# Matmuls that take their moving columns alternately from two halves

## The chip, the core and the metric

The kernel runs on one core of one Trainium2 chip. The metric is the device time of one execution in microseconds (us); the median of several runs is compared. TensorE (PE) does matrix products: a stationary operand of up to 128 x 128 (the weights here) is loaded, a moving operand (the activations here) streams past it column by column, and the result goes to PSUM, which has eight banks of 512 fp32 columns. VectorE (DVE) and ScalarE (ACT) read PSUM banks and read and write SBUF. GpSimd (POOL) and SyncE (SP) mostly issue transfers.

## What is computed

One inference step of a decoder with two layers, for a prompt of 512 positions and for 8 samples of one position each. All 520 positions go through the same weights, so they are handled together. Cut to what matters here:

```
def _swiglu(x, wg, wu, wd):
    return (jax.nn.silu(x @ wg) * (x @ wu)) @ wd          # 1024 -> 2816 -> 1024

for l in range(DEPTH):                                     # DEPTH = 2
    if l == N_A_LAYERS:                                    # after the first layer
        kv = _rmsnorm(x, kv_norm_g) @ w_kv                 # shared keys and values
    x = x + 0.5 * _swiglu(_rmsnorm(x, norm_g[l, 0]), ...)
    h = _rmsnorm(x, norm_g[l, 1])
    x = x + (pooling mixer(h) if l < N_A_LAYERS else window attention(h @ w_q) @ w_o)
    x = x + 0.5 * _swiglu(_rmsnorm(x, norm_g[l, 2]), ...)
y = _rmsnorm(x, final_norm_g)
```

There are four feed-forward blocks. They hold most of the arithmetic.

## The kernel before

**Layout.** Activations lie transposed: 128 features on the partitions, the 520 positions (`TOK`) as columns in the free dimension, eight such tiles for 1024 features. `H` is 260, half of the columns; `hcols(t, 0)` and `hcols(t, 1)` are the first and the second 260 columns of a tile. A pair of PSUM banks (`duo()`) takes a tile of 520 results, 260 in each bank, and `halves(t)` views an SBUF tile in the same two halves.

**Products.** Every operand is split into a high and a low part of type fp32r, and each product is the sum of three matmuls: high by high, low by high, high by low (`terms`). Two helpers issue nearly all of them:

- `mm` (matmuls at L604) multiplies one block of 128 x 128 weights with one activation tile, three terms by two halves of 260 columns. It serves the plain tiles, the projections of queries, keys, values and outputs, and the plain down products.
- `product` (matmuls at L632) multiplies four blocks of weights with four pieces of 260 columns, twelve matmuls into one bank. It serves the Strassen-like form, in which a block of products over two halves of the features and two halves of the columns is made from seven products of sums, not from eight.

In both, the moving operand `b` is a run of 260 adjacent fp32r columns in SBUF, the result a run of 260 adjacent columns at the start of a bank (`bank[:, :H]`). The names of the moving operands in the profile are `xh`/`xl`, `th`/`tl`, `hh`/`hl` and `ph`/`pl` (high and low parts), those of the split weights `wh`/`wl`, those of the banks `ps`. Some products do not go through these helpers: the pooling mixer (L1193, L1238), the attention scores and values (L1533, L1618), the tail of the last block (264 columns at L1970, 384 at L1977) and transposes (L1880, L1591 and others).

**Who reads the banks.** In `plain_end` VectorE multiplies gate sums by the norm factor `R` (L751), ScalarE applies silu, and VectorE multiplies with the up sums (L753). In `strassen_tile` ScalarE copies intermediate sums (`sa`, `sb`: L775, L780, L783) and VectorE adds and multiplies from banks (L787, L793, L798); `strassen_down` does likewise (L812 to L838). `add` inside `ffn` (L908) adds a plain down product to the residual, `o_add` (L1761) the output projection, `rope` and `q_evac` (L1474) copy keys and queries, L1376 the values.

**Order.** Weights are loaded in chunks by SP's and POOL's queues, split by ScalarE (`wh`, L287) and VectorE (`wl`, L288), and prefetched a few pieces ahead (`Weights`). Outside the attention part, where a written plan sets the order, a scheduler places the instructions of each engine.

Of the kernel before, what the change touches and what calls it, by code (L numbers as in the profile page):

```python
# [324 lines left out]
def yoco_step(ctx, tc, ins, outs):  # L325
# [212 lines left out]
    def halves(t):  # L538
        return t.rearrange("p (h c) -> p h c", h=2)

# [59 lines left out]
    def mm(w, kk, mov, banks, first, last, halves=(0, 1), pin=seq, between=None):  # L600

        for i, (a, b) in enumerate(terms(w, mov)):
            for hf in halves:
                ins = T.matmul(  # L604
                    banks[:, hf, :H],
                    a[:, kk, :],
                    hcols(b, hf),
                    start=(first and i == 0),
                    stop=(last and i == 2),
                )  # L610
                pin(ins)
            if between is not None and i < 2:
                between()
# [11 lines left out]
    def product(mov, bank, more=False):  # L625


        w = W.get()
        W.prefetch()
        for kk in range(4):  # L630
            for i, (a, b) in enumerate(terms(w, mov[kk])):
                T.matmul(  # L632
                    bank[:, :H],
                    a[:, kk, :],
                    b,
                    start=(not more and kk == 0 and i == 0),
                    stop=(kk == 3 and i == 2),
                    skip_group_check=more,
                )
# [95 lines left out]
    def plain_end(tmp, pg, pu, hs):  # L735
# [3 lines left out]
        if not there[0]:  # L739
            S.copy(halves(g), pg[:, :, :H])  # L740
            S.copy(halves(t), pu[:, :, :H])

# [7 lines left out]
        else:  # L750
            V.tensor_tensor(halves(g), pg[:, :, :H], halves(R), op=ALU.mult)  # L751
            S.activation(t, g, AF.Silu)
            V.scalar_tensor_tensor(halves(g), pu[:, :, :H], -1.0, halves(t), op0=ALU.mult, op1=ALU.mult)  # L753
            hidden(g, hs)
# [7 lines left out]
    def strassen_tile(tmp, xx, tt, hs, early=False):  # L762
# [11 lines left out]
        product(B(xx, lo, 0), a)  # L774
        S.copy(hcols(sa, 0), a[:, :H])  # L775
# [4 lines left out]
        S.copy(sb, b[:, :H])  # L780
        finish()
        product(B(tt, lo, 1), a, True)
        S.copy(hcols(sa, 1), a[:, :H])  # L783
# [3 lines left out]
        V.tensor_tensor(halves(g), halves(sa), c[:, :, :H], op=ALU.add)  # L787
        if early:
# [3 lines left out]
        product(B(tt, up, 0), a, True)  # L792
        V.tensor_tensor(sb, sb, a[:, :H], op=ALU.add)  # L793

        def rest():
            V.tensor_tensor(hcols(g, 1), sb, hcols(t, 1), op=ALU.mult)
            product(B(tt, up, 1), a, True)
            V.tensor_tensor(hcols(g, 0), a[:, :H], hcols(t, 0), op=ALU.mult)  # L798
            hidden(g, hs)
# [3 lines left out]
    def strassen_down(tmp, hs):  # L803
# [3 lines left out]
        def head(i):  # L807
# [3 lines left out]
            product(b["B11"], a)  # L811
            S.copy(hcols(sa, 0), a[:, :H])  # L812
            product(b["T1"], c[:, 1, :])
            S.copy(sb, c[:, 1, :H])
            st[i] = a, c, sa, sb

        def second(i):
            a, c, sa, sb = st[i]
            product(b["T2"], a, True)
            S.copy(hcols(sa, 1), a[:, :H])  # L820

        def third(i):
# [3 lines left out]
            u = tmp.tile([P, TOK], F32, tag="u", name="u", bufs=nu[0])  # L826
            V.tensor_tensor(halves(u), halves(sa), c[:, :, :H], op=ALU.add)
# [3 lines left out]
            V.tensor_tensor(sb, sb, a[:, :H], op=ALU.add)  # L831

        def rest(i):
# [3 lines left out]
            product(b["T4"], a, True)  # L837
            V.tensor_tensor(hcols(u, 0), a[:, :H], hcols(R, 0), op=ALU.mult)  # L838
            V.scalar_tensor_tensor(x[2 * i + 1], u, 0.5, x[2 * i + 1], op0=ALU.mult, op1=ALU.add)
# [39 lines left out]
    def ffn(fi, tmp, mov, hooks, tt, tags, after, before_last=None, first=None, by_parts=None, hold=False):  # L879

        j = 0
        for pi, n in enumerate(PARTS):
# [20 lines left out]
            def add(m, bank, hfs):  # L903
                c = slice(hfs[0] * H, (hfs[-1] + 1) * H)
                u = tmp.tile([P, TOK], F32, tag="u", name="u", bufs=nu[0])[:, c]
                parts = lambda z: z.rearrange("p (h c) -> p h c", c=H)
                pin = later if last and hold and m >= PIN0 else seq
                pin(V.tensor_tensor(parts(u), bank[:, hfs[0] : hfs[-1] + 1, :H], parts(R[:, c]), op=ALU.mult))  # L908
                pin(V.scalar_tensor_tensor(x[m][:, c], u, -0.5, x[m][:, c], op0=ALU.mult, op1=ALU.add))
# [407 lines left out]
    def rope(out, banks, cosr, sinr, pool, tags):  # L1317
# [3 lines left out]
        sw = pool.tile([P, TOK], F32, tag=tags[1], name="rp1", bufs=n)  # L1321
        S.copy(halves(raw), banks[:, :, :H])
        V.tensor_tensor(out, raw, cosr, op=ALU.mult)
# [5 lines left out]
    with ff_pool() as tmp:  # L1329
# [45 lines left out]
        for g in range(2):  # L1375
            V.tensor_tensor(halves(vT[g]), vb[g][:, :, :H], halves(R), op=ALU.mult)  # L1376

# [70 lines left out]
    with tc.tile_pool(name="at", bufs=2, reuse_waits="tile") as at:  # L1448
# [22 lines left out]
        def q_evac(t):  # L1471

            qraw[t] = big.tile([P, TOK], F32, tag="th", name="qraw")
            later(S.copy(halves(qraw[t]), qb[t][:, :, :H]))  # L1474

# [283 lines left out]
        def o_add(n):  # L1759
            half, m = n // KT, n % KT  # L1760
            later(V.tensor_tensor(halves(x[m]), parts.pop((half, m))[:, :, :H], halves(x[m]), op=ALU.add))  # L1761

# [333 lines left out]
```

## Time and profile before

| | |
|---|---|
| median of 3 runs | 1617.17 us (1616.67 to 1617.82) |
| span of the profiled execution, first to last instruction | 1614.7 us |
| own time of the profiled execution beyond its span | not given apart; the median lies 2.5 us above the span |
| TensorE | 1599.9 us busy, 13338 matmuls |
| weight loads of TensorE | 1589.5 us, 13338 |
| VectorE | 1417.0 us |
| ScalarE | 976.4 us |
| GpSimd | 310.0 us |

Matmuls overlap in a pipeline, so their printed durations (some 283 ns) are longer than the distance from one to the next; the distance is read from the chain of work in order of time. "PEld" is the weight load, which overlaps the matmul before it. A row of a group gives line, engine, operation, output <- inputs, shapes and count, then busy time and the mean duration in ns, then the idle time of the engine just before and who ended it.

### The profile page before, as it was taken

To read this page: it belongs to the slowest core of one execution; us is meant where nothing else is said; L and a number is where in the kernel's file an instruction comes from. 1 tells how busy PE (TensorE), PEld (TensorE's weight loads), DVE (VectorE), ACT (ScalarE), POOL (GpSimd) and SP (SyncE) were. 2 spreads that over 40 slices of the span, in tenths; PEclk is the share of its full clock that TensorE was granted. 3 is DMA by queue.
4 is the path that set the end of the run, shared out by engine and by line. 5 is a ranking of instruction groups with operands and counts; after the bars stand their busy time and mean duration, and the time that the engine had idled before them with its cause. 6 is when DMAs were issued, how large, how long until landed. Compare 5 with 4: busy or idle time off the path is not lost.

```text
span 1614.7 us, 35073 instructions
## 1 busy us (share of the span) xinstructions
PE 1599.9 (99%) x13338; PEld 1589.5 (98%) x13338; DVE 1417.0 (88%) x2783; ACT 976.4 (60%) x2030; POOL 310.0 (19%) x348
## 2 busy tenths in 40 slices
PE   9999999999999999999999999999999999999997
PEld 9999999999999999999999999999999999999997
DVE  6999999879999999978899999877787999999976
ACT  5765665657665665655565565555786665565555
POOL 1122222101121221100312222200461122222200
PEclk9999999999999999999999999999999999999999
DMA  9588888654687888735788878853333588888941
GB/s 236 115 187 184 181 180 189 162 171 119 131 188 169 186 182 182 168 114 120 192 175 180 189 172 181 193 159 90 67 85 91 121 169 184 185 183 182 190 123 54
DMA packets 420037, 255.43 MB, mean 158 GB/s; under 512 B 13182, under 2 KB 400246, under 8 KB 419828
## 3 DMA queue, kind: packets, MB, share of 16 engines
q1 hardware_dynamic: 339918, 187.56, 42.0%
q0 software_dynamic: 76192, 60.53, 26.1%
q10 hardware_dynamic: 3758, 5.09, 1.0%
q8 instruction: 105, 1.72, 0.4%
q14 instruction: 64, 0.52, 0.1%
HBM read 218.59 MB, written 6.11 MB: 139 GB/s over the span
## 4 chain that ended last, share of the span: by engine, by line
PE 98%; DVE 1%; ACT 0%; POOL 0%; issue 0%; DVEq 0%; ACTq 0%; POOLq 0%
PE ps L632 68%; PE ps L604 23%; PE pv L1618 1%; PE pv L1193 1%; PE pv L1591 1%; PE pv L1238 1%; PE ps L1533 1%; PE ps L1970 0%; PE ps L1977 0%; PE ps L1065 0%; PE ps L560 0%; PE pv L1724 0%; PE ps L1074 0%; ACT wh L287 0%; PE ps L1880 0%; PE pv L1678 0%
## 5 line engine op out<-in xcount | busy, mean ns | idle before, releaser
L287 ACT ACTIVATE wh<-raw 128x512 fp32r<-128x512 f32 (+1 forms) x770 | 449.2, 619 | 260.9 <-PE ps L632 76.9
L288 DVE TENSOR_TENSOR wl<-raw,wh 128x512 fp32r<-128x512 f32 (+1 forms) x770 | 500.8, 674 | 58.8 <-ACT wh L287 57.5
L632 PE MATMUL ps<-th,wh 128*128 128x260 f32 x1232 | 347.3, 283 | 0.4 <-ACT sb L780 0.4
L632 PE MATMUL ps<-tl,wh 128*128 128x260 f32 x1232 | 347.1, 283 | 0.0
L632 PE MATMUL ps<-th,wl 128*128 128x260 f32 x1232 | 345.8, 282 | 0.0
L632 PE MATMUL ps<-xh,wh 128*128 128x260 f32 x908 | 255.4, 283 | 0.8 <-ACT wh L287 0.7
L632 PE MATMUL ps<-xl,wh 128*128 128x260 f32 x908 | 254.6, 282 | 0.0
L632 PE MATMUL ps<-xh,wl 128*128 128x260 f32 x908 | 254.2, 282 | 0.0
L632 PEld LDWEIGHTS ps<-th,wh 128*128 128x128 f32 x1232 | 231.9, 188 | 1.1 <-ACT sb L780 0.6
L632 PEld LDWEIGHTS ps<-tl,wh 128*128 128x128 f32 x1232 | 231.8, 188 | 0.0
L632 PEld LDWEIGHTS ps<-th,wl 128*128 128x128 f32 x1232 | 231.1, 188 | 0.0
L398 POOL DMA_DIRECT2D S<-in_ffn_w_up_dram x77 | 102.2, 1327 | 472.6 <-DMA S<-in_ffn_w_up_dram 139.4
L632 PE MATMUL ps<-hh,wh 128*128 128x260 f32 x656 | 183.9, 283 | 1.6 <-ACT wh L287 0.7
L632 PE MATMUL ps<-hl,wh 128*128 128x260 f32 x656 | 184.1, 283 | 0.0
L632 PE MATMUL ps<-hh,wl 128*128 128x260 f32 x656 | 183.2, 282 | 0.0
L214 POOL DMA_DIRECT2D raw<-raw x109 | 96.2, 882 | 401.2 <-DVE wl L288 127.2
L632 PEld LDWEIGHTS ps<-xh,wh 128*128 128x128 f32 x908 | 170.4, 188 | 1.6 <-ACT wh L287 1.6
L632 PEld LDWEIGHTS ps<-xl,wh 128*128 128x128 f32 x908 | 170.6, 188 | 0.0
L632 PEld LDWEIGHTS ps<-xh,wl 128*128 128x128 f32 x908 | 170.4, 188 | 0.0
L632 PEld LDWEIGHTS ps<-hh,wh 128*128 128x128 f32 x656 | 122.9, 188 | 2.7 <-ACT wh L287 1.1
L632 PEld LDWEIGHTS ps<-hl,wh 128*128 128x128 f32 x656 | 123.2, 188 | 0.1
L632 PEld LDWEIGHTS ps<-hh,wl 128*128 128x128 f32 x656 | 122.9, 188 | 0.0
(369 smaller groups left out, 3639.8 us busy)
## 6 DMA issues: line engine op xcount, KB each, us to landing
raw<-in_ffn_w_gate_dram SPq DMA_DIRECT2D x87, 512.0 KB, 4.4
raw<-in_ffn_w_up_dram SPq DMA_DIRECT2D x87, 512.0 KB, 5.9
raw<-in_ffn_w_down_dram SPq DMA_DIRECT2D x128, 256.0 KB, 4.8
raw<-raw POOLq DMA_DIRECT2D x109, 256.0 KB, 3.8
S<-in_ffn_w_up_dram SPq DMA_DIRECT2D x77, 256.0 KB, 4.2
S<-in_ffn_w_up_dram POOLq DMA_DIRECT2D x77, 256.0 KB, 5.4
raw<-in_ffn_w_down_dram SPq DMA_DIRECT2D x16, 768.0 KB, 4.4
S<-in_ffn_w_down_dram SPq DMA_DIRECT2D x32, 256.0 KB, 3.2
```

The lines of the kernel that those rows point to most:

```text
L214: G.dma_start(blk(raw, 2, 1), blk(raw, 1, 1), accum_op=ALU.add)
L287: pin(nc.scalar.activation(dh, src, AF.Copy))
L288: pin(nc.vector.tensor_tensor(dl, src, dh.bitcast(F32), op=ALU.subtract))
L398: return [ld(lambda t: t, a), lambda t: nc.gpsimd.dma_start(t, b, accum_op=ALU.add)]
L604: ins = T.matmul(banks[:, hf, :H], a[:, kk, :], hcols(b, hf), start=(first and i == 0), stop=(last and i == 2),)
L632: T.matmul(bank[:, :H], a[:, kk, :], b, start=(not more and kk == 0 and i == 0), stop=(kk == 3 and i == 2), skip_group_check=more,)
L1193: later(T.matmul(o, a[:, c], b[:, kk, :], start=(n == 0), stop=(n == 5)))
L1238: later(T.matmul(o, zz[tau][z][:, c], b, start=(i == 0), stop=(i == len(lst) - 1)))
L1533: later(T.matmul(o, q_[rows, qc], k_[rows, kc_], start=(i == 0), stop=(i == 2)))
L1591: later(T.transpose(self.both[bi][:, kt * 256 + e * P : kt * 256 + (e + 1) * P], z, ident))
L1618: later(T.matmul(o, a, p_[:, kc_], start=(n == 0), stop=(n == 3 * len(kts) - 1)))
```

## The change

The products of `mm` and `product` take their moving columns in another order: column 0, 130, 1, 131 and so on of the 260, through a view of two dimensions (`two`). Their results still go to 260 adjacent columns of a bank, so result column 2a + b belongs to position 130b + a. All readers of these banks take them back in the order of positions: they read the bank with a step of two columns, first the even and then the odd ones (`outs` for a pair of banks, `out` for one), and write SBUF in the usual order; `back` and the new `halves` give the SBUF views the matching dimensions. Products outside the two helpers are as before.

```
 def halves(t):
-    return t.rearrange("p (h c) -> p h c", h=2)
+    return t.rearrange("p (h b a) -> p h b a", h=2, b=2)
+
+def two(z):
+    return z.rearrange("p (b a) -> p a b", b=2)
+
+def back(z):
+    return z.rearrange("p (b a) -> p b a", b=2)
+
+def outs(banks):
+    return banks[:, :, :H].rearrange("p h (a b) -> p h b a", b=2)
+
+def out(bank):
+    return bank[:, :H].rearrange("p (a b) -> p b a", b=2)
...
     # mm
                     banks[:, hf, :H],
                     a[:, kk, :],
-                    hcols(b, hf),
+                    two(hcols(b, hf)),
...
     # product
                     bank[:, :H],
                     a[:, kk, :],
-                    b,
+                    two(b),
...
     # plain_end
-            V.tensor_tensor(halves(g), pg[:, :, :H], halves(R), op=ALU.mult)
+            V.tensor_tensor(halves(g), outs(pg), halves(R), op=ALU.mult)
             S.activation(t, g, AF.Silu)
-            V.scalar_tensor_tensor(halves(g), pu[:, :, :H], -1.0, halves(t), op0=ALU.mult, op1=ALU.mult)
+            for hf in range(2):
+                V.scalar_tensor_tensor(
+                    back(hcols(g, hf)), out(pu[:, hf, :]), -1.0, back(hcols(t, hf)), op0=ALU.mult, op1=ALU.mult
+                )
...
     # strassen_tile
-        S.copy(hcols(sa, 0), a[:, :H])
+        S.copy(back(hcols(sa, 0)), out(a))
...
-        V.tensor_tensor(halves(g), halves(sa), c[:, :, :H], op=ALU.add)
+        V.tensor_tensor(halves(g), halves(sa), outs(c), op=ALU.add)
...
-        V.tensor_tensor(sb, sb, a[:, :H], op=ALU.add)
+        V.tensor_tensor(back(sb), back(sb), out(a), op=ALU.add)
```

The other readers of these banks (`strassen_down`, `add`, `rope`, the values, `q_evac`, `o_add`) change in the same way.

The instructions are the same in kind and number but for one: the product at L753 (`scalar_tensor_tensor`) is issued as two of 260 columns each. On VectorE, at the end of the third plain tile of the first feed-forward block (`g` is the gate tile, `t` its silu, `wl` the low part of a piece of weights, `xa`/`xb` and `t_...` the sums for the Strassen form), the rows before are:

```order
L288 TENSOR_TENSOR wl<-raw_362,wh 128x512
L751 TENSOR_TENSOR g<-ps_584,R 128x520
L380 TENSOR_TENSOR pl<-t_634,ph 128x520
L227 TENSOR_TENSOR raw_362<-raw_362 128x512
L873 TENSOR_TENSOR t_681<-xb,xa 128x260
L874 SCALAR_TENSOR_TENSOR t_681<-t_680,xb 128x260
L753 SCALAR_TENSOR_TENSOR g<-ps_585,t 128x520
```

The same place on VectorE after the change:

```order
L288 TENSOR_TENSOR wl<-raw_362,wh 128x512
L767 TENSOR_TENSOR g<-ps_584,R 128x520
L380 TENSOR_TENSOR pl<-t_634,ph 128x520
L227 TENSOR_TENSOR raw_362<-raw_362 128x512
L892 TENSOR_TENSOR t_681<-xb,xa 128x260
L893 SCALAR_TENSOR_TENSOR t_681<-t_680,xb 128x260
L770 SCALAR_TENSOR_TENSOR g<-ps_585,t 128x260 x2
```

The order stands; the last row has become two instructions of half the size.

The scheduler also places some ready instructions of neighbouring tiles in another order. The largest such place on TensorE lies in the Strassen tiles of the last feed-forward block (the numbers after `ps` name pairs of banks, and those of after are 8 higher for the same pair). Before:

```order
L632 MATMUL ps_18284<-th,wh 128x260
L632 MATMUL ps_18284<-tl,wh 128x260
L632 MATMUL ps_18284<-th,wl 128x260
L632 MATMUL ps_18403<-xh,wh 128x260
L632 MATMUL ps_18403<-xl,wh 128x260
L632 MATMUL ps_18545<-xh,wh 128x260
L632 MATMUL ps_18545<-xl,wh 128x260
L632 MATMUL ps_18403<-xh,wl 128x260
```

And in the changed kernel, at the place where the products for the pair 18411 end and the last products for the pair 18292 have not begun:

```order
L648 MATMUL ps_18411<-xh,wh 128x260
L648 MATMUL ps_18411<-xl,wh 128x260
L648 MATMUL ps_18410<-th,wh 128x260
L648 MATMUL ps_18410<-tl,wh 128x260
L648 MATMUL ps_18411<-xh,wl 128x260
```

Twelve matmuls into an older bank (18284, later 18292), which stood ahead of the end of the product into 18403 (now 18411), now stand behind it, and the first two of a product into 18410 have come ahead of that end. SP and POOL issue the same instructions in the same order as before.

More of the change, by code (lines that the diff above doesn't have):

```diff
@@ L819, in second @@
             product(b["T2"], a, True)
-            S.copy(hcols(sa, 1), a[:, :H])
+            S.copy(back(hcols(sa, 1)), out(a))
         def third(i):
@@ L1321, in rope @@
         sw = pool.tile([P, TOK], F32, tag=tags[1], name="rp1", bufs=n)
-        S.copy(halves(raw), banks[:, :, :H])
+        S.copy(halves(raw), outs(banks))
         V.tensor_tensor(out, raw, cosr, op=ALU.mult)
@@ L1473, in q_evac @@
             qraw[t] = big.tile([P, TOK], F32, tag="th", name="qraw")
-            later(S.copy(halves(qraw[t]), qb[t][:, :, :H]))
+            later(S.copy(halves(qraw[t]), outs(qb[t])))
         def q_gather(t, e):
```

27 lines of the change are left out of this document (13 added, 14 removed).

## The prediction

> **What bounds the kernel now.** I read the engines' shares first, then the chain of work that ended last, then the groups of instructions, then the chain in order of time at a few places, and last the busy time by stage.
>
> ```profile
> span 1614.7 us, 35073 instructions
> PE 1599.9 (99%) x13338; PEld 1589.5 (98%) x13338; DVE 1417.0 (88%) x2783; ACT 976.4 (60%) x2030; POOL 310.0 (19%) x348
> PEclk9999999999999999999999999999999999999999
> PE 98%; DVE 1%; ACT 0%; POOL 0%; issue 0%; DVEq 0%; ACTq 0%; POOLq 0%
> ```
>
> TensorE is busy in all but 14.8 us of the span, at a granted clock of nine tenths or more in every slice, and it is 98% of the chain. So the time is the number of matmuls times the distance from one matmul to the next. The busy sum cannot give that distance, since matmuls overlap: the groups below print 283 ns each. Their counts are of use. Each row stands for one of three terms with the same count (high by high, low by high, high by low part).
>
> ```profile
> L632 PE MATMUL ps<-th,wh 128*128 128x260 f32 x1232 | 347.3, 283 | 0.4 <-ACT sb L780 0.4
> L632 PE MATMUL ps<-xh,wh 128*128 128x260 f32 x908 | 255.4, 283 | 0.8 <-ACT wh L287 0.7
> L632 PE MATMUL ps<-hh,wh 128*128 128x260 f32 x656 | 183.9, 283 | 1.6 <-ACT wh L287 0.7 <-ACT hh L379 0.5 <-ACT sa L812 0.4
> L632 PE MATMUL ps<-ph,wh 128*128 128x260 f32 x256 | 72.7, 284 | 0.0
> L604 PE MATMUL ps<-hh,wh 128*128 128x260 f32 x572 | 116.5, 286 | 0.8 <-DVE g L751 0.6 <-DVE nm L1552 0.2
> L604 PE MATMUL ps<-xh,wh 128*128 128x260 f32 x448 | 91.1, 286 | 0.0
> ```
>
> That is 3 x (1232 + 908 + 656 + 256 + 572 + 448) = 12216 matmuls of 260 columns, of 13338 in all. These are the ones whose moving operand changes. The last column shows that they hardly wait for anyone: 3.6 us over these rows.
>
> The distance comes from the chain in order of time (start, length, what, how many):
>
> ```profile
> 108.12 143.90 PE ps L632 x1195
> 1579.12 4.30 PE ps L604 x36
> 1583.41 0.44 PE ps L1880 x4
> 1589.45 2.19 PE ps L1970 x18
> 1598.21 3.13 PE ps L1977 x18
> ```
>
> In the long stretch a matmul of 260 columns comes every 143.90/1195 = 120.4 ns (a few records may be missing, so it is a little less), in the short one every 119.4 ns. Those of 264 columns (L1970) take 121.7 ns, those of 384 columns (L1977) 173.9 ns. One more column thus costs (173.9 - 121.7)/120 = 0.435 ns, and 260 columns cost 113.1 of the 119.4 ns; the other 6.3 ns do not depend on columns. The transposes of 128 columns (L1880) come every 110 ns, not at half the distance: something apart from the columns, which goes with each matmul and its load of weights, keeps them 110 ns apart. The kernel is bounded by the rate at which columns stream, with that second floor 9.4 ns below.
>
> **The change part by part.** Counts of matmuls, columns, weight loads and transfers stay: nothing on POOL or SP moves, and the matmuls still write 260 adjacent columns of a bank.
>
> *The moving read.* Each of the 12216 matmuls now reads column 0, 130, 1, 131 and so on, with 520 bytes from one column to its partner and back. This is the term that decides, since every nanosecond on the distance is 12.2 us of the kernel. No large matmul of the trace reads its moving columns with a step. The nearest rows on TensorE are two groups of 8 columns, the first read with a step of 32 bytes (`qz[g][:, :, :, b]`), the second side by side (`prT`):
>
> ```profile
> 1178.31 0.95 PE L1678 MATMUL pv<-qz,kc 128*128 128x8 f32 x8
> 1188.50 0.95 PE L1724 MATMUL pv<-prT,vc 128*128 128x8 f32 x8
> ```
>
> Eight of either take 0.95 us, so the step costs nothing that can be seen. But that is weak: 8 columns are little beside the 110 ns floor, and a doubled column would hide under it. Bounds: below, a product cannot come closer than the 110 ns of the transposes, a gain of 9.4 ns or 12216 x 9.4 ns = 115 us. Above, if two adjacent columns are now fetched together and an alternating pair is not, a column costs twice 0.435 ns: 113.1 ns more on each, 1382 us. I take 0, the value of the only rows that compare a stepped with an unstepped read on this engine.
>
> [...]
>
> *The reads of the banks.* VectorE and ScalarE now read PSUM with a step of two columns and write SBUF as before. VectorE's groups that do so, and two of ScalarE's:
>
> ```profile
> L787 DVE TENSOR_TENSOR g<-sa,ps 128x520 f32<-128x520 f32 x77 | 53.1, 690 | 5.4 <-PE ps L632 4.8
> L793 DVE TENSOR_TENSOR sb<-sb,ps 128x260 f32<-128x260 f32 x77 | 32.1, 417 | 2.4 <-PE ps L632 2.4
> L798 DVE TENSOR_TENSOR g<-ps,t 128x260 f32<-128x260 f32 x77 | 32.7, 425 | 15.4 <-PE ps L632 14.4
> L827 DVE TENSOR_TENSOR u<-sa,ps 128x520 f32<-128x520 f32 x32 | 22.0, 688 | 3.5 <-ACT sa L820 2.0 <-PE ps L632 1.5
> L831 DVE TENSOR_TENSOR sb<-sb,ps 128x260 f32<-128x260 f32 x32 | 13.4, 417 | 0.4 <-PE ps L632 0.4
> L838 DVE TENSOR_TENSOR u<-ps,R 128x260 f32<-128x260 f32 x32 | 13.6, 425 | 9.6 <-PE ps L632 9.4
> L908 DVE TENSOR_TENSOR u<-ps,R 128x520 f32<-128x520 f32 x29 | 20.0, 691 | 11.2 <-PE ps L604 11.2
> L1761 DVE TENSOR_TENSOR x<-ps,x 128x520 f32<-128x520 f32 x16 | 11.1, 694 | 6.3 <-PE ps L604 6.2
> L751 DVE TENSOR_TENSOR g<-ps,R 128x520 f32<-128x520 f32 x8 | 5.5, 696 | 2.7 <-PE ps L604 1.9 <-PE ps L1393 0.6
> L753 DVE SCALAR_TENSOR_TENSOR g<-ps,t 128x520 f32<-128x520 f32 x8 | 5.5, 693 | 3.1 <-PE ps L604 3.1
> L775 ACT COPY sa<-ps 128x260 f32<-128x260 f32 x77 | 28.8, 374 | 81.9 <-PE ps L632 81.5
> L1474 ACT COPY qraw<-ps 128x520 f32<-128x520 f32 x8 | 4.8, 594 | 9.6 <-PE ps L604 9.6
> ```
>
> VectorE takes (690 - 417)/260 = 1.05 ns per element, ScalarE (594 - 374)/260 = 0.85 ns, each slower than TensorE's column. One small copy of the trace does read PSUM with a step, of 64 bytes; beside it stand neighbours of 8 and 32 elements that read theirs side by side:
>
> ```profile
> L1746 DVE TENSOR_TENSOR hl<-oS,hh 128x8 fp32r<-128x8 f32 x8 | 1.2, 156 | 0.0
> L1731 DVE COPY oS<-pv 64x16 f32<-64x16 f32 x8 | 1.0, 168 | 0.2 <-PE pv L1724 0.2
> L1683 DVE TENSOR_TENSOR sT<-pv,rs 128x32 f32<-128x32 f32 x4 | 0.7, 183 | 0.0
> ```
>
> From 8 to 32 elements the time grows by 27 ns, so 16 elements would take 165 ns; the stepped copy takes 168. A doubled element would have added some 17 ns. So I take 0 here too, between no gain (the engine already takes an element at its own pace) and a doubled element: (77 + 32 + 29 + 16 + 8 + 8) x 520 + (77 + 77 + 32 + 32) x 260 = 145080 elements, at 1.05 ns 152 us more of VectorE. ScalarE has 40% of the span free and cannot become the bound by this.
>
> *The split product.* The instruction at L753 becomes two of 260 elements at some 425 ns (L798): 8 x (850 - 693) = 1.3 us more of VectorE. It follows the gate and up products of a plain tile, and TensorE already has the next tile's products to run, so most is hidden; uncovered it would be 1.3 us. I take 0.5.
>
> *The order.* VectorE, ScalarE and TensorE have small local swaps where ready instructions of neighbouring tiles interleave in another way; weights come through the same queues in the same order. I take 0, between -2 and 2 us: 3.6 us is all that the products' rows above show as waits. Should a swap uncover something, the split weights (`wh` from ScalarE) would be late next.
>
> Sum: 1614.7 + 0 + 0 + 0.5 + 0 = 1615.2 us for the span. The median of the runs, 1617.17, lies 2.5 us above the profiled span (start and end around it), which gives 1617.7, say 1618.
>
> **The rivals.** First, *each alternating column is a fetch of its own*: slower. Place: every matmul at L604 and L632. It decides once TensorE's reader cannot hold both halves at once; a column would need to cost only 0.001 ns more to show in the time. For it: TensorE's 0.435 ns per column is half or less of what VectorE (1.05) or ScalarE (0.85) needs for an element, so it may well be getting two adjacent columns per fetch. Against it: only the 8-column rows. With a doubled column it gives 1614.7 + 1382 + 2.5 = 2999 us; at ScalarE's pace, 260 x (0.85 - 0.435) = 107.9 ns, it gives 1614.7 + 1318 + 2.5 = 2935; at VectorE's, 159.9 ns, 3570. I put it at 2935 to 3000. [...]
>
> Second, *two places at once stream faster*: the 6.3 ns besides the columns, or part of the column time, may be a conflict at one place of the memory that alternation spreads out. For it: 260 columns stand 9.4 ns above the distance of the transposes. Against it: long stretches with quite different transfers hold the same distance (120.4 ns above, 119.4 in the tail), so no conflict is seen. Half of the 9.4 ns gives 12216 x 4.7 ns = 57 us, so 1560; all of it 1503, and VectorE would begin to bound before that, as these stages show (length, TensorE, weight loads, VectorE, ScalarE, POOL):
>
> ```profile
> 109.00:252.00 143.00, 143.00 (x1190) 142.59 (x1189) 133.50 (x246) 83.08 (x171) 29.77 (x28) 1.00 0.85 181
> 483.00:627.00 144.00, 143.99 (x1196) 143.58 (x1196) 134.44 (x248) 84.07 (x173) 30.62 (x28) 1.00 0.84 178
> 786.00:873.00 87.00, 86.99 (x727) 86.72 (x725) 80.56 (x150) 53.02 (x108) 17.49 (x16) 1.00 0.77 167
> 1282.00:1369.00 87.00, 86.99 (x725) 86.73 (x724) 82.93 (x158) 53.55 (x110) 18.45 (x18) 1.00 0.78 170
> ```
>
> Third, *VectorE becomes the bound by the stepped banks*: slower. With the 152 us spread like its work (10.7%), it needs 147.8, 148.8, 89.2 and 91.8 us in these stages of 143, 144, 87 and 87: 4.8 + 4.8 + 2.2 + 4.8 = 17 us, so 1634. It decides from about 5% more VectorE time in the last of them. The stepped copy above speaks against it. [...]
>
> **How the numbers follow.** Chances: no effect on the column rate 0.45, each column a fetch of its own 0.28, faster streaming 0.19, VectorE as the bound 0.08. A change under 0.2% (3.2 us) cannot be told from none. Within the first case, swaps and small effects of the steps leave 0.28 within 0.2%, 0.06 faster and 0.11 slower; its own range is 1612 to 1624. Faster is 0.06 + 0.19 = 0.25, same 0.28, slower 0.11 + 0.28 + 0.08 = 0.47. So the likeliest single case is no change, though slower as a whole is likelier than either other sign. For 8 in 10 the range must reach the doubled column, 3000, and half of the streaming gain, to 1550; left out are larger gains (about 0.07) and costlier columns (about 0.08).
>
> **What the changed kernel's profile would show.** For the forecast: 1195 matmuls at the product line again in about 144 us, the groups of bank reads at 690, 417 and 425 ns, 8 more VectorE instructions. For the first rival: the same matmuls 220 ns or more apart, VectorE's and ScalarE's shares nearly halved with unchanged durations. For the second: under 119 ns, and longer waits of TensorE for `wh` and `g`. For the third: bank reads near 1240 and 690 ns, and TensorE waiting for VectorE. A distance between 121 and 200 ns would mean that a switch costs something of its own, which none of my prices has.

## The result and the profile after

The changed kernel takes 1532.83 us (median of 4 runs, 1532.24 to 1535.35) against 1616.92 us for the kernel before (4 runs): a ratio of 0.9483, 95% interval 0.947 to 0.9497, or 84.1 us less. The prediction was 1618 us, with 1550 to 3000 as its range. The time lies below the range, and on the side that the prediction held least likely.

The page of the changed kernel, its span and its engines, and the shares of the chain that ended last:

```profile
span 1530.5 us, 35121 instructions
PE 1507.7 (99%) x13338; PEld 1492.0 (97%) x13338; DVE 1406.7 (92%) x2791; ACT 969.2 (63%) x2030; POOL 309.6 (20%) x348
PE 24%; DVE 3%; ACT 1%; DMA 1%; issue 1%; POOL 0%; SPq 0%; DVEq 0%; ACTq 0%; POOLq 0%
```

TensorE has the same 13338 matmuls in 92.2 us less of busy time, and its idle time has grown from 14.8 to 22.8 us. VectorE has gone from 88% to 92% of the span. The chain of before was matmuls nearly throughout (98%). Followed back from the end, the chain of now loses its thread inside the span, so that the shares shown add up to some 30% only; the pieces that are left show short waits for VectorE, ScalarE and a transfer between long runs of matmuls.

The chain of the changed kernel in order of time (start, length, what, how many):

```profile
1412.00 65.48 PE ps L648 x584
1495.64 4.02 PE ps L620 x36
1505.43 2.19 PE ps L1988 x18
1514.18 3.16 PE ps L1995 x18
```

L648 and L620 are the lines of `product` and `mm` after the change. Their matmuls of 260 columns come every 65.48/584 = 112.1 ns, or 4.02/36 = 111.7 ns in the tail; before it was 119.4 ns there (and 120.4 in the long stretch). The matmuls that the change does not touch are as before: 264 columns (L1988) in 121.7 ns. So 260 alternating columns now take 10 ns less than 264 columns side by side, in the same kernel, a few microseconds apart. By the distance in the tail the change is worth 12216 x (119.4 - 111.7) = 94 us. The tail is a little quicker than the rest, though. Worked out from the starts of all 12216 matmuls in the two traces, with stops of 150 ns and more left out, the distance is 119.8 ns before and 111.7 ns after: 8.1 ns, or 99 us in all. Of these 99 us, 84 arrived; where the other 15 went is taken up under e6.

The readers of the banks, with the row of products that waits most, answer to the groups shown before:

```profile
L806 DVE TENSOR_TENSOR g<-sa,ps 128x520 f32<-128x520 f32 x77 | 53.5, 695 | 1.1 <-PE ps L648 0.8
L812 DVE TENSOR_TENSOR sb<-sb,ps 128x260 f32<-128x260 f32 x77 | 32.6, 424 | 0.0
L817 DVE TENSOR_TENSOR g<-ps,t 128x260 f32<-128x260 f32 x77 | 32.8, 426 | 6.5 <-PE ps L648 6.4
L770 DVE SCALAR_TENSOR_TENSOR g<-ps,t 128x260 f32<-128x260 f32 x16 | 6.1, 427 | 1.5 <-PE ps L620 1.5
L794 ACT COPY sa<-ps 128x260 f32<-128x260 f32 x77 | 28.4, 369 | 58.3 <-PE ps L648 57.7 <-DVE t L892 0.4
L648 PE MATMUL ps<-hh,wh 128*128 128x260 f32 x656 | 180.1, 278 | 3.5 <-ACT wh L287 1.7 <-DVE g L817 0.6 <-ACT hh L379 0.5
```

Reading a bank with a step of two columns costs VectorE 695, 424 and 426 ns where it was 690, 417 and 425, and ScalarE 369 ns where it was 374. What has changed is the last column. The idle time of VectorE ahead of its reads is down from 5.4, 2.4 and 15.4 us to 1.1, 0.0 and 6.5 us: it hardly waits for TensorE any more. TensorE waits more instead: 3.5 us ahead of the `hh`, `wh` products, where it was 1.6 us.

The stages say the same (length, TensorE, weight loads, VectorE, ScalarE, POOL, then granted clock, share of the DMA engines, GB/s):

```profile
109.00:250.00 141.00, 140.96 (x1253) 140.16 (x1252) 138.57 (x257) 83.50 (x171) 31.48 (x29) 1.00 0.90 193
1196.00:1294.00 98.00, 95.79 (x849) 94.94 (x848) 96.36 (x197) 64.11 (x128) 19.58 (x20) 1.00 0.80 176
```

VectorE is busy 98% of both stages, where it was busy 93% and 95% of the first and the last stage shown in the prediction, and in the second TensorE idles 2.2 us.

### The profile page after: what moved, and what is told of

It reads as the page before. It is cut to its first block, busy times and chain, and to the rows that moved or that the text cites. A ratio compares the mean times of both kernels' runs of the same rounds, so it can differ in the third digit from the quotient of the medians.

```text
span 1530.5 us, 35121 instructions
## 1 busy us (share of the span) xinstructions
PE 1507.7 (99%) x13338; PEld 1492.0 (97%) x13338; DVE 1406.7 (92%) x2791; ACT 969.2 (63%) x2030; POOL 309.6 (20%) x348
## 5 line engine op out<-in xcount | busy, mean ns | idle before, releaser
L648 PE MATMUL ps<-th,wh 128*128 128x260 f32 x1232 | 338.5, 276 | 0.6 <-ACT sb L799 0.4
L648 PE MATMUL ps<-th,wl 128*128 128x260 f32 x1232 | 337.2, 275 | 0.5 <-DVE wl L288 0.5
L648 PE MATMUL ps<-tl,wh 128*128 128x260 f32 x1232 | 337.6, 275 | 0.0
L648 PE MATMUL ps<-xh,wh 128*128 128x260 f32 x908 | 248.8, 276 | 1.2 <-ACT wh L287 0.9
L648 PE MATMUL ps<-xh,wl 128*128 128x260 f32 x908 | 248.3, 275 | 0.5 <-DVE wl L288 0.4
L648 PE MATMUL ps<-xl,wh 128*128 128x260 f32 x908 | 248.2, 275 | 0.0
L648 PEld LDWEIGHTS ps<-th,wh 128*128 128x128 f32 x1232 | 234.0, 190 | 2.0 <-ACT wh L287 0.9
L648 PEld LDWEIGHTS ps<-tl,wh 128*128 128x128 f32 x1232 | 234.1, 190 | 0.0
L648 PEld LDWEIGHTS ps<-th,wl 128*128 128x128 f32 x1232 | 233.3, 190 | 0.7 <-DVE wl L288 0.7
L648 PE MATMUL ps<-hh,wh 128*128 128x260 f32 x656 | 180.1, 278 | 3.5 <-ACT wh L287 1.7
L648 PE MATMUL ps<-hl,wh 128*128 128x260 f32 x656 | 179.2, 276 | 0.9 <-DVE hl L380 0.9
L648 PE MATMUL ps<-hh,wl 128*128 128x260 f32 x656 | 178.3, 275 | 0.0
L648 PEld LDWEIGHTS ps<-xh,wh 128*128 128x128 f32 x908 | 172.2, 190 | 2.2 <-ACT wh L287 1.5
L648 PEld LDWEIGHTS ps<-xh,wl 128*128 128x128 f32 x908 | 171.9, 190 | 1.0 <-DVE wl L288 1.0
L648 PEld LDWEIGHTS ps<-xl,wh 128*128 128x128 f32 x908 | 172.2, 190 | 0.1
L648 PEld LDWEIGHTS ps<-hh,wh 128*128 128x128 f32 x656 | 124.0, 190 | 5.5 <-ACT wh L287 2.3
L648 PEld LDWEIGHTS ps<-hl,wh 128*128 128x128 f32 x656 | 124.2, 190 | 1.6 <-DVE hl L380 1.6
L648 PEld LDWEIGHTS ps<-hh,wl 128*128 128x128 f32 x656 | 123.9, 190 | 0.0
```

Source lines behind the costliest of these rows:

```text
L648: T.matmul(bank[:, :H], a[:, kk, :], two(b), start=(not more and kk == 0 and i == 0), stop=(kk == 3 and i == 2), skip_group_check=more,)
```

## The experiments

**What is to be settled.** My theory after the result: a stream of adjacent fp32r columns runs below the rate that TensorE can take, and two places at once let it reach that rate; the bank reads, the split product and the new order are worth nothing; about 10 us of the gain went back because VectorE became the bound at places. Rivals: the stream suffered from the other engines' accesses to the memory; the gain comes from the bank reads or the order; the load of the weights is what the alternation relieves.

Four of the runs (e1, e3, e7, e9) are kernels of their own that compute nothing of the reference: after the loads, streams of 96 matmuls with nothing else running, each stream with one shape and one form of moving operand, on a line of its own, and each matmul with a load of weights of its own. The distance is the length of a stream in the chain, divided by 96. Each of the four was executed once; rows that recur in several of them agree (512 columns: 228.2, 228.2 and 228.4 ns side by side, 217.0 ns alternating in e1, e3 and e7).

**e1: the distance by itself.** The forms, for `n` columns of a tile `m`:

```
m[:, :n]                                                # side by side
m[:, :n].rearrange("p (b a) -> p a b", b=2)             # alternating (as the change has it)
m[:, :n].rearrange("p (b a) -> p a b", b=4)             # four places in turn
m[:, :n].rearrange("p (b a r) -> p a b r", b=2, r=r)    # alternating runs of r columns
m[:, :n].rearrange("p (a b) -> p b a", b=2)             # step of two: even columns, then odd ones
```

> This kernel leaves out the whole decoder step and writes zeros; it only issues streams of 96 matmuls, each with its own weights, nothing else running, one stream per line. Wanted is the distance from one matmul to the next. Side by side, the trace of before gives 119.4 ns at 260 columns, 173.9 at 384 and, with its 0.435 ns per column, 229.6 at 512. Theory A (adjacent columns cost more per column, alternating ones less): the 7.7 ns gained at 260 grow with the columns, to 11.4 ns at 384 and 15.2 at 512 (214.4 ns). Theory B (the fixed 6.3 ns at the start of a stream shrink): the gain is 6 to 8 ns at 260, 384 and 512 alike (221.9 at 512). Theory C (alternating columns stream much faster, and at 260 columns the floor of 110 ns that goes with each load of weights takes over): the gain at 512 is well over 15.2 ns, under 210 ns. Rival to all three (conflict with the reads and writes of other engines, which alternation evades): with the other engines idle, side by side is as fast as alternating, both near 112 ns at 260. Of the patterns at 512 columns: if what matters is that neighbours in the stream are not neighbours in memory, even columns first and then odd ones, a step of two columns, and a step of eight are all as fast as alternating, and alternating in runs of two or four adjacent columns is slow or half way; if two places are needed, only the alternating ones gain.

The chain of e1: 260 columns side by side (L59) and alternating (L60), 512 (L63, L64), 512 with a step of two (L69), in runs of two and of four (L70, L71), bf16 alternating (L76), and fp32r from four places in turn (L83):

```profile
21.39 11.50 PE bank L59 x96
33.23 10.83 PE bank L60 x96
...
77.53 21.91 PE bank L63 x96
99.78 20.83 PE bank L64 x96
165.62 43.66 PE bank L69 x96
209.62 32.10 PE bank L70 x96
242.06 24.12 PE bank L71 x96
375.86 46.53 PE bank L76 x96
540.59 27.28 PE bank L83 x96
```

Side by side and alternating take 119.8 and 112.8 ns at 260 columns, 174.5 and 163.6 at 384 (16.75 and 15.71 us a stream), 228.2 and 217.0 at 512. Here no other engine works, and 7.0 of the kernel's 8.1 ns at 260 columns are there: the rival of a conflict with other engines falls, but for at most the last 1 ns (for which the starts are another candidate, see e9). The differences of 7.0, 10.9 and 11.2 ns go neither quite by theory A nor by B; e7 and e9 take that up. With 128 and 200 columns both forms take 112 to 113 ns. How far apart the two places lie hardly matters: halves 257 to 272 columns apart give 217.0 to 217.8 ns. It matters much which stepped form is used: a step of two columns takes 454.8 ns for 512 columns, twice as long, and a step of eight 432.1; runs of two 334.4, runs of four 251.3; four places 284.2; bf16 alternating 484.7 ns where bf16 side by side goes at 216.0 ns.

**e2: the banks alone.** The kernel after the change with all its bank reads, its split product and its order, but with the moving columns side by side (the readers then take the columns in another order than they were made):

```
 def two(z):
-    return z.rearrange("p (b a) -> p a b", b=2)
+    return z
```

> The changed kernel with its moving columns side by side again, the banks still read with a step of two (so that positions of the results are permuted). If the whole gain comes from the moving read: the time of before, 1617 us within 4, and bank reads at 690 and 417 to 425 ns. If the stepped bank reads or the changed order bring a part of it: below 1610. If the stepped reads cost something that the gain hides: above 1621.

1617.57 us against 1616.26, ratio 1.0008 (0.9999 to 1.0018). Its groups and one piece of its chain:

```profile
L806 DVE TENSOR_TENSOR g<-sa,ps 128x520 f32<-128x520 f32 x77 | 53.3, 693 | 6.6 <-PE ps L648 6.0
L812 DVE TENSOR_TENSOR sb<-sb,ps 128x260 f32<-128x260 f32 x77 | 32.3, 421 | 2.0 <-PE ps L648 2.0
1063.98 4.32 PE ps L648 x36
```

The bank reads take 693 and 421 ns, the distance is 4.32/36 = 120 ns as before. So the parts of the change other than the moving read are worth nothing that can be measured, and the whole gain comes from the moving read.

**e3: which steps are fast.** More forms on 512 columns: alternating with a step of two or of four inside each half, a start moved by two columns, each column twice, runs of eight, lengths from 208 to 288, and plain fp32, which runs as two matmul instructions each (192 for 96 in the rows below).

> Again only streams of 96 matmuls with zeros as the outputs; the decoder step is left out. From the first set of streams, at 512 columns: side by side 228 ns, alternating 217, step of two columns 454, step of eight 432, alternating in runs of two 334, in runs of four 251, over four places 284. Theory R2 (the stream is taken two columns at a time, and what counts is whether the next column but one lies in the same short run of memory as the last but one): alternating with a step of two columns within each half is like side by side, about 228; with a step of four, no column near the last but one, 430 to 455; alternating written with three dimensions (two blocks of 2 x 128) 217; each column taken twice in a row, 217 or less; runs of eight between side by side and runs of four, 228 to 251. Theory R1 (one reader that can hold two places open; runs of two and four were slow because a third dimension of the view costs time): three dimensions over 300 ns, runs of eight about 250 too. Theory R0 (two neighbours of the stream must not lie in the same 8 bytes): each column taken twice is as slow as side by side or slower. On the floor: side by side leaves it where 0.43 ns per column plus 8 to 11 ns pass 112 ns, between 224 and 256 columns; alternating stays at 112 ns up to 256 and grows by 0.417 ns per column beyond 260. Starting the run one or three columns later costs about 9 ns, two columns later nothing. In fp32 without rounding the two orders differ by less than 2%.

The chain of e3: step of two within alternating halves (L60), step of four within them (L61), side by side from column 2 (L63), fp32 of 128 columns side by side and alternating (L80, L81):

```profile
67.24 21.89 PE bank L60 x96
89.47 43.66 PE bank L61 x96
154.64 22.52 PE bank L63 x96
405.61 21.55 PE bank L80 x192
427.49 26.34 PE bank L81 x192
```

The theory called R2 there gave the times of the stepped forms in advance: 228.0 ns for the step of two inside alternating halves (as slow as side by side, not twice as slow), 454.8 for the step of four, 217.0 for columns taken twice, 244.4 for runs of eight. So it is not a step as such that costs: with two places in turn a step of two inside each is free of the doubling that it has alone. The expectations on the start and on fp32 failed. Side by side, a start two columns later costs 6.4 ns (234.6 from column 2, 228.2 from column 0), not nothing, and one three columns later 1.8 ns (230.0), not 9; and plain fp32 loses by alternating (22% at 128 columns, 27% at 256), not under 2%. By length, the two forms part between 240 columns (112.8 and 112.7 ns) and 256 (121.0 and 112.8).

**e4 and e5: each helper alone.** One keeps `two` in `mm` only, the other in `product` only; all readers stay as in the changed kernel, and so take the columns of the other helper in another order.

```
                     a[:, kk, :],                         # e4: in product; e5: the same in mm
-                    two(b),
+                    b,
```

> Only the 3060 matmuls of the helper mm alternate; those of product take their columns side by side (their results are then permuted, since the banks are read with a step of two in both). If each alternating matmul gains 7.6 ns wherever it stands: 1617 - 23 = 1594. If the gain needs the dense stages of product: over 1605.

> Only the 9156 matmuls of product alternate, those of mm do not. At 7.6 ns each: 1617 - 70 = 1547 if nothing is given back; if the stages of product, where VectorE was busy for 93 to 95% of the time, give back the whole of the 8 to 10 us that the full change lacks, 1555 to 1557.

e4: 1596.19 us, ratio 0.988 (0.9863 to 0.9896), 20 us less. e5: 1554.03 us, ratio 0.9612 (0.9598 to 0.9627), 62 us less. Two pieces from the chain of e4, then two from that of e5:

```profile
1540.05 4.33 PE ps L648 x36
1558.16 4.02 PE ps L620 x36
```

```profile
665.64 4.02 PE ps L648 x36
1043.73 4.31 PE ps L620 x36
```

In each kernel the line that alternates stands at 111.7 ns and the other at 120. The gains add up, 20 + 62 = 82 us of 84, and each is below its count by 8.1 ns: 3 x (572 + 448) x 8.1 ns = 24.8 us for `mm`, 9156 x 8.1 = 74.2 us for `product`. Both expectations that nothing is given back (1594 and 1547 us) were thus missed, by 2 and 7 us.

**e6 and e11: what VectorE took back.** Both leave out the third sum of the Strassen weights (109 additions on VectorE, 75 us by its row; VectorE's busy time, in which overlapping instructions count once, falls by 55 us from the changed kernel to e6), so their sums are not the reference's: e6 from the changed kernel, e11 from the kernel before.

```
             s2(raw)
-            V.tensor_tensor(blk(raw, 1, 2), blk(raw, 1, 2), blk(raw, 1, 1), op=ALU.add)
             return blk(raw, 1, 2)
```

> The changed kernel without the third sum of weights on VectorE (L227, 109 x 0.68 us), so those products are with other weights. Theory (what the change lacks to 12216 x 7.6 = 93 us was given back as waits for VectorE): with 74 us less of VectorE's work the time falls by those 8 to 10 us, to 1523 to 1526. Rival (the gain per matmul is all there is, VectorE's share does not matter): 1532 to 1533.

> The kernel before (moving columns side by side) without the third sum of the weights (L227, 109 additions on VectorE, 74 us of its work), so its output is not the reference's. It is the control for the changed kernel without that sum, which gained 12.2 us. If those 12 us are time that the faster products gave back to VectorE, the kernel before, whose TensorE idles 14.8 us in all and waits 3.6 us in the products, gains little: 0 to 4 us, 1612 to 1616. Rival: the sum costs its 12 us in either kernel (its place in the chain from load to split weight counts, not VectorE's share), and this run takes about 1604 us.

e6 takes 1520.61 us, ratio 0.9407 (0.9393 to 0.9421); e11 takes 1612.26 us, ratio 0.9976 (0.9967 to 0.9985). The pages of e6 and of e11:

```profile
span 1516.3 us, 34951 instructions
PE 1499.0 (99%) x13338; PEld 1489.8 (98%) x13338; DVE 1352.0 (89%) x2682; ACT 991.7 (65%) x2030; POOL 309.8 (20%) x348
```

```profile
span 1610.3 us, 34946 instructions
PE 1597.1 (99%) x13338; PEld 1589.0 (99%) x13338; DVE 1370.9 (85%) x2674; ACT 996.2 (62%) x2030; POOL 309.8 (19%) x348
```

Less VectorE work is worth 12.2 us in the changed kernel and 4 us in the kernel before, so some 8 us of it are there only because TensorE has become faster. Without the control I would have put all 12 us down to the change. The kernels without the sum differ by 1612.26 - 1520.61 = 91.7 us, where the distance gives 99; with the sum it is 84.1.

The starts of the matmuls in the profiled executions show the same. For each of the 12216 matmuls the time to the next start is taken; the distance is the mean of those under 150 ns, and the rest are stops.

| | distance | stops of 150 ns and more | their time beyond the distance |
|---|---|---|---|
| before | 119.8 ns | 90 | 12.7 us |
| changed | 111.7 ns | 152 | 26.4 us |
| before, without the sum (e11) | 119.8 ns | 57 | 6.7 us |
| changed, without the sum (e6) | 111.7 ns | 69 | 9.5 us |

So 13.7 of the 15 us that are missing went into longer stops of TensorE, and without the third sum the change adds only 2.8 us of them. The way from sum to stop can be seen on ScalarE: its split `wh` waits for VectorE's sums of the weights (L221 and L227) for 76.6 + 31.8 us before and 80.5 + 50.2 us in the changed kernel, but for 9.4 us in e6. How much of this hangs on VectorE's share of the time and how much on the sum's place on the way from load to split weight is not told apart, since leaving the sum out changes both.

**e7: is it the load of the weights?** The streams of e1 with weights of 128, 64 and 32 columns, with the same weights again and again, with weights that lie two columns apart, and with starts from column 4 to 8.

> Streams of 96 matmuls with zeros as the outputs; the decoder step is left out. So far the distance of alternating matmuls is 3.6 ns plus 0.417 ns per column from 272 columns on, that of matmuls side by side 9 to 11 ns more, nearly the same at 272, 384 and 512 columns: a cost per matmul, not per column. Theory W (the reads of the moving columns meet the reads of the next weights, which take a fixed number of columns; the order that returns to a place leaves room for them): with 64 columns of weights the gap at 512 and 384 halves to 4 to 7 ns, with 32 it is 1 to 4 ns. Theory S (a cost of starting or ending a stream side by side): the gap stays 9 to 12 ns with 128, 64 and 32 columns of weights. On the floor of 112 ns at 128 moving columns: if it is the load of 128 columns of weights, it falls with 64 (to 57 to 70 ns) and 32; weights with a step of two columns raise it, towards 200 ns, if weights are read as moving columns are. Starting a run of 512 four or eight columns later is like starting it at 0 (228 ns), five like one (238). Moving operands that change from matmul to matmul behave as one that stays: 228 and 217, 120 and 113 ns.

The chain of e7: 128 moving columns with 64 weight columns side by side and alternating (L70, L71), with 32 weight columns (L76, L77); then 512 columns from columns 5 and 7 (L85, L87) with 128 weight columns:

```profile
208.72 5.81 PE bank L70 x96
214.92 5.65 PE bank L71 x96
297.63 5.79 PE bank L76 x96
303.81 5.39 PE bank L77 x96
443.23 22.76 PE bank L85 x96
489.18 21.87 PE bank L87 x96
```

The floor is the load: 128 moving columns take 112 ns with 128 weight columns, but 60.5 and 58.9 with 64. Weights that lie two columns apart raise it to 118.4 ns, and the 260 alternating columns with it, from 112.8 to 118.9. The difference between the two forms is not the load: with 32 weight columns, where 128 columns alternating come at 56.1 ns and the load is thus no longer than that, 512 columns still take 231.8 and 216.1 ns, and 128 columns now show a difference too (60.3 and 56.1 ns). So the theory of a clash with the weight load, W, falls. Columns side by side depend on the start, from 227.8 (column 7) to 237.1 ns (column 5) in these rows, with 232.8 to 234.5 from columns 4, 6 and 8, where 228 was expected from 4 and 8, and 237.6 from column 1 (e1). Alternating takes 217.8 from column 1 (e3), against 217.0.

**e9: a cost per column or per matmul?** The two forms at seven lengths with 32 weight columns and at five with 128, the start changing from matmul to matmul; and bf16.

> Streams of 96 matmuls with nothing else running, so the distance is the length of a stream divided by 96. First group: weights of 32 columns, lengths 128, 192, 256, 320, 384, 448, 512, each side by side and alternating between its two halves, the first column changing from matmul to matmul over eight places. Second group: weights of 128 columns, lengths 260, 320, 384, 448, 512. Theory A (side by side, each column costs 0.03 ns more than alternating): the difference grows in proportion to the columns, about 4, 6, 8, 10, 12, 14, 16 ns in the first group, and 7, 10, 12, 14, 16 ns in the second, where at 260 the 112 ns floor hides part of it. Rival S (a fixed cost per matmul, which two places at once avoid): the difference is the same at 256 as at 512, between 9 and 16 ns, in both groups. Third group, bf16 of 512 columns: side by side, alternating, alternating runs of two and of four, even columns before odd ones, and the first column moved by one. If a fetch carries four bytes (two bf16 columns), runs of two bf16 columns go about as one fp32r column does when alternating, 217 to 230 ns; if what counts is the number of columns and not their bytes, runs of two take about 334 ns and runs of four 251 ns, as with fp32r.

The chain of e9, in pairs of side by side and alternating: 128 columns (L62, L63), 512 (L74, L75), all with 32 weight columns; 260 with 128 weight columns (L76, L77); then bf16 of 512 columns in runs of two (L88) and with a step of two (L90):

```profile
33.40 5.86 PE bank L62 x96
39.66 5.46 PE bank L63 x96
184.93 22.20 PE bank L74 x96
207.46 20.82 PE bank L75 x96
228.62 11.78 PE bank L76 x96
240.74 10.83 PE bank L77 x96
463.93 26.05 PE bank L88 x96
512.44 21.70 PE bank L90 x96
```

The difference is 4.2 ns at 128 columns, 8.3 at 256 (11.38 and 10.58 us a stream), 14.4 at 512: it grows with the columns, as theory A has it, so the fixed cost (rival S) falls. From 128 to 512 columns, alternating adds (20.82 - 5.46)/96/384 = 0.417 ns per column, side by side 0.443. At 260 columns with full weights it is 9.9 ns when the starts change, more than the 7 expected. With 128 weight columns the growth is less even: 12.0, 12.3, 13.5 and 15.7 ns at 320, 384, 448 and 512 columns. The bf16 rows went by neither expectation: runs of two take 271.4 ns (not 217 to 230, nor 334), runs of four 226.9 and a step of two 226.0, against 484.7 alternating.

**e8: the sum on GpSimd.** Since VectorE is busy for 92% of the span and POOL for 20%, the third sum was moved to GpSimd.

```
-            V.tensor_tensor(blk(raw, 1, 2), blk(raw, 1, 2), blk(raw, 1, 1), op=ALU.add)
+            G.tensor_tensor(blk(raw, 1, 2), blk(raw, 1, 2), blk(raw, 1, 1), op=ALU.add)
```

> The changed kernel with the third sum of weights (L227, 109 times 128 x 512) on GpSimd in place of VectorE; all results as in the reference. Without that sum the time was 1520.6 us. If GpSimd, busy 20% of the time, does each sum in 2 us or less beside its transfers and without slowing VectorE: 1520 to 1526. Rival (GpSimd's sums hold up the transfers queued behind them on its queue, so that raw and S come late, or the two engines slow each other): 1533 or more.

1653.39 us, ratio 1.023 (1.0216 to 1.0244): 121 us slower than the changed kernel. The group of the sums, and a row of the waits (who waits for whom: us in total, times, longest):

```profile
L227 POOL TENSOR_TENSOR raw<-raw 128x512 f32<-128x512 f32 x109 | 182.9, 1678 | 124.7 <-DVE wl L288 124.7
ACT wh L287 <- POOL raw L227: 179.4, 96, 5.0
```

A sum takes 1678 ns there against 692 on VectorE, and ScalarE's split of the weights stands and waits for it, 179 us in all. A part of the loss is the clock: the granted clock was 0.985 on the mean, where it was 0.999 in the changed kernel, an estimate of 1651.6 x 0.014 = 23 us. A step on the way from load to split weight is not free merely because its engine has time.

**e10: the other products too.** The changed kernel with `two` also in the attention values, the pooling mixer and the tail.

> The changed kernel in which the products outside the two helpers alternate as well, their readers adapted: 168 matmuls of 256 columns (attention values), 120 of 256 (pooling mixer), 54 of 264 and 36 of 384 (tail). By the distances measured alone (121.0 against 112.8 ns at 256, about 9 ns at 264, 174.5 against 163.6 ns at 384) it gains (168 + 120) x 8.2 + 54 x 9 + 36 x 11 ns = 3.2 us if TensorE is what bounds there, so about 1529 to 1530 us. Rival: these places wait for VectorE or ScalarE (softmax, mixer), and only the 90 of the tail show, 0.9 us: 1531.5 to 1532.5.

1532.21 us (1529.4 to 1532.95), ratio 0.9473 (0.946 to 0.9486), not to be told from the changed kernel's 0.9483. The chain in its tail:

```profile
1506.05 2.03 PE ps L1990 x18
1514.33 2.93 PE ps L1997 x18
```

264 columns now take 112.8 ns (121.7 before) and 384 take 162.8 (175.6), and by the starts of the matmuls the mixer and the attention values go from 118 to 112 ns, so the form works in those products as well. Whether the time follows is open. Three of the five runs took 1532.2 to 1533.0 us, as the rival has it, and two 1529.4 and 1529.5, as the first expectation has it. The profiled execution is one of the three; in it the granted clock was 0.66 from 1127 to 1132 us, in the attention part (1.00 there in the changed kernel; 0.98 on the mean from 1097 to 1168 us), which is some 5 x 0.34 = 1.7 us by itself. No version was found that is clearly faster than the changed kernel.

## Why the prediction was wrong

- **The step that failed** is "The moving read … I take 0". It measured 119.8 - 111.7 = 8.1 ns less on each of 12216 matmuls, 99 us (7.7 ns and 94 us by the tail). The lower bound, "a gain of 9.4 ns or … 115 us" down to the floor of the transposes, held and was nearly reached: the distance now stands 1.7 ns above that floor. The value of 0 came from two groups of 8 columns, which the text itself called weak, since the floor hides any effect there; by e7 that floor is the load of 128 weight columns (112 ns for 128 moving columns, against 60.5 and 58.9 with 64 weight columns).
- **What the profile could have told.** I used the 0.435 ns per column of the tail as if it were TensorE's own rate. Nothing in the trace said that it was; e9 shows 0.417 ns alternating. The distance of the transposes, 110 ns, bounded the gain but did not say whether columns can stream faster than in the tail. A stream by itself says it: 119.8 ns side by side and 112.8 alternating at 260 columns (e1).
- **The second rival** is what happened, in its second form: the column time fell (e9), not the 6.3 ns beside it. That a conflict at one place of the memory is the reason is not shown. My argument against it, that long stretches with different transfers hold the same distance, speaks against a conflict with other traffic, and e1 leaves room for 1 ns of it at most; but the loss lay inside the stream, where such a comparison cannot see it. Its price, half of the 9.4 ns, was too small: 8.1 of 9.4. That VectorE "would begin to bound before" the whole gain held in the main: of the 15 us between 99 and 84, some 8 hang on a sum of VectorE's (e6, e11), and the causes of the others were not traced. The range, at 1550, ended just below this price of 1560, and so missed the time by 17 us.
- **The first rival** is a real behaviour in other forms: at 512 columns a step of two fp32r columns doubles the time (454.8 ns against 228.2 side by side), four places cost 284.2, bf16 alternating 484.7 against 216.0. For two places of fp32r it does not hold (217.0).
- **The third rival** did not happen: e2 puts bank reads, split product and order together at a ratio of 1.0008. With a step of two columns in PSUM, VectorE takes 693 to 695 and 421 to 424 ns where it took 690 and 417, and ScalarE 369 ns where it took 374: no doubled element.
- **The split product**: the durations add up to 16 x 427 ns = 6.8 us where L753 took 8 x 693 ns = 5.5, the 1.3 us of the prediction; the two halves overlap, so that busy time grew by 0.6 us only (6.1 against 5.5). It is hidden as supposed (e2). **The order**: 0, right.
- **What would show it**: the sign named for the second rival, a distance under 119 ns and longer waits of TensorE for `wh` and `g`, is what the profile after shows.

## What to carry to other kernels

When matmuls bound a kernel, compare their distance with the best that any row or a stream by itself reaches, before taking the present distance as the engine's rate; here 6% (119.8 against 111.7 ns, 99 us of 1617) hid in the order of the columns, and a free view of the moving operand took them. Measure the exact form and type: of the stepped forms tried in fp32r, alternation of two places was the fastest and a plain step of two cost double (217.0 and 454.8 ns against 228.2 side by side), and alternation lost in bf16 (484.7 against 216.0 ns) and in plain fp32 (by 22% and 27%). Then look who is next: of 99 us, 15 were lost again, some 8 of them to VectorE's sums on the way to the split weights, and only a control, the kernel before without the same sum, told them from what leaving it out is worth anyway.

## What the hardware showed unexpectedly

- Adjacent fp32r columns stream at 0.443 ns each (e9, 32 weight columns), and their time depends on where the tile starts (227.8 to 237.6 ns for 512 columns); alternating ones at 0.417 ns, with hardly a difference by start (217.0 and 217.8). Why two places are served better than one was not found. A reader that takes two columns at a time, the idea of R2, gave the stepped fp32r forms of e3 in advance, but it does not say why runs of two (334.4) and four places (284.2) lie between whole and double, nor does it give the times in bf16 or the dependence on the start.
- A matmul of fp32r with a load of its own of 128 weight columns does not come closer than 112 ns in these streams (111.7 in the kernel, whose transposes come at 110). With 64 weight columns 128 alternating columns come at 58.9 ns, and at 56.1 with 32, so the floor with 64 lies at 59 ns or below.
- At 260 columns both limits nearly meet: alternating, a stream costs 217.0 - 512 x 0.417 = 3.5 ns beside its columns, so 260 x 0.417 + 3.5 = 112 ns, and the load takes 112 ns. A faster stream or a faster load alone should then bring this kernel's products nothing more; that was not tried, but weights two columns apart, with their floor of 118 ns, show at once (118.9 ns in e7).
